# The ring of stored token sums in the down projection: laid out by product, each product's tile fetched after its slot's last product

## The chip, the core and the metric

The kernel runs on one core of a Trainium2 chip. The metric is the device time of one execution in microseconds (us). Three runs of the kernel before took 2399.78, 2400.1 and 2400.78 us; the median is 2400.1 us. Nothing runs on the other cores.

## The reference

One layer of a hybrid decoder trunk is applied to 512 prompt tokens and 8 x 4 sample tokens, in float32, with a model width of 2048 and a hidden width of 8192. The change lies in the MLP, and only there:

```python
h = rms_norm(x, norm_ffn_w[l])
x = x + jnp.square(jax.nn.relu(h @ w_up[l])) @ w_down[l]
```

Ahead of it stands a mixer (a short gated convolution beside a gated delta rule, each behind a large input projection), and behind it a final norm. The 544 token columns are handled as two halves of 272 (`HT`).

## The kernel before

**Numbers.** TensorE (PE) multiplies in a rounded float32 form. So each float32 operand is split into a rounded part `hi` (on ScalarE, ACT) and the rest `lo` (on VectorE, DVE), and each product takes three matmuls: `w_hi` with `x_hi`, `w_hi` with `x_lo`, `w_lo` with `x_hi`. Every matmul there is 128 x 128 by 272 columns.

**Two by two blocks with seven products.** Most of the MLP is done in 2 x 2 blocks in the manner of Strassen and Winograd: two weight blocks by two, times two token halves, with 7 block products in the place of 8. A `Pair` holds the four weight quarters of a block (`w_q`, one DMA each on the queue of SyncE, SP) and builds the sums of weights for the products 6, 5, 7, 3 and 4 on DVE (lines 1118 to 1125). The products run in the order 1, 2, 6, 5, 7, 3, 4 (`ORDER`). For the last sum that the pair needs, `w_s` at line 1120, the quarters `a21` and `a22` must have landed. The weight parts are made two products ahead of PE (`ahead`). An engine works its own instructions in order; the order of the instructions on each engine is set when the kernel is built.

**Way up and way back.** On the way up, each of 32 hidden blocks `m` gives a tile `u` of four parts. For the 28 blocks in `KS` (m from 3 to 30), `keep_sums` makes the seven token sums that the seven products of the way back need, splits each into `hi` and `lo`, and writes all fourteen columns of 272 to a DRAM tensor `ucd{m}`, by four DMAs on the queue of GpSimd (POOL): two for three sums, two for four (lines 1179 and 1180). `T_AT` gives the position `b`, from 0 to 6, of the sum of each product.

On the way back, 42 visits go over the 8 output blocks `m`. A visit multiplies up to six (`SPAN`) consecutive blocks `j` of `KS` into one output block. So a visit of six is 7 products x 6 blocks x 3 matmuls = 126 matmuls. Within a product, PE goes through the blocks `j` in order, the lowest first. Each product's result is added to the output by DVE (line 927).

**The ring.** Only 8 blocks' sums (`RING`) are held in SBUF at a time, seven tiles of 128 x 544 each (`uc`). Where a visit is the last that uses a block `j`, block `j + 8` is fetched into its slots. `last_use` says which visit that is; it is ten visits that fetch, two blocks each. Before the change, the tensor lies as seven `hi` columns and then seven `lo` columns, and tile `b` of a block holds the columns 2b and 2b+1. So one tile serves two products (the `hi` of the products 1 and 3, say), or the `hi` of one and the `lo` of another. The seven DMAs of both blocks are written in the program behind the visit's last product, 4. What waits in fact is each DMA by itself, until PE has read the slot that it fills for the last time. POOL's queue carries nothing else in that part.

**Beginning and end of the ring.** The blocks 0 and 1 are fetched during the last block of the way up (line 1216), the blocks 2 to 7 right behind it (line 1273). Then come eight plain products (`Plain`, hidden block pairs kept aside), four ahead of the first visit and one within each of the first four. Behind the last visit two stored blocks are done with plain products, with their tiles `ux` loaded by SP.

Of the kernel before, what the change touches and what calls it, by code (L numbers as in the profile page):

```python
# [9 lines left out]
F32 = mybir.dt.float32  # L10
# [8 lines left out]
P = 128  # L19
# [38 lines left out]
def trunk(ctx, tc, a):  # L58
# [921 lines left out]
    x2_d = [tile_in(dram, f"x2d{i}", [P, 2, 2, HT]) for i in range(KT // 2)]  # L980
    u_d = {m: tile_in(dram, f"ud{m}", [P, 4, HT]) for m in STORED}
    u0_d = [tile_in(dram, f"u0d{m}", [P, 2, 4, HT]) for m in KEPT]
    uc_d = {m: tile_in(dram, f"ucd{m}", [P, 14, HT]) for m in range(N_PLAIN, NF - 1)}

    first_part(KT - 1, lambda: None)
    ln_exp(True)
# [184 lines left out]
    def keep_sums(m, u):  # L1171

        t = t_tile("tc", "T")
        sums(t, u[:, 1], u[:, 0], u[:, 3], u[:, 2])
        d = uc_d[m]
        for src, at, n in ((u[:, 1:4], 0, 3), (t, 3, 4)):
            hi = t_tile("u_hi", "hi", F32R)[:, :n]
            parts_into(hi, src.bitcast(F32R), src)
            nc.gpsimd.dma_start(d[:, at : at + n], hi.bitcast(F32))
            nc.gpsimd.dma_start(d[:, 7 + at : 7 + at + n], src)  # L1180

    u_0, x2v = [], []

# [5 lines left out]
    def block_out(m):  # L1189
        u = t_tile("u", "u")  # L1190

        def out(p, ps):
            with urgent():
                if p in (1, 6, 5):
                    S.activation(u[:, {1: 1, 6: 0, 5: 2}[p]], ps, AF.Copy)
                elif p == 4:
                    S.activation(u[:, 3], ps, AF.Relu)
                    S.activation(u, u, AF.Square)
                else:
                    d = u[:, {2: 1, 7: 2, 3: 0}[p]]  # L1200
                    V.tensor_tensor(d, d, ps, ADD)
                if p == 3:
                    S.activation(u[:, 0:3], u[:, 0:3], AF.Relu)
            if p == 4 and m in STORED:
                nc.gpsimd.dma_start(u_d[m], u)
            elif p == 4:
                keep_sums(m, u)
            if p == 1 and m == NF - 1:
                residual(range(4), nc.sync)
            if p == 2 and m == NF - 1:  # L1210
                for i in range(4):
                    parts = [c_tile(hlp, "u0") for _ in range(2)]
                    for j in range(2):
                        nc.sync.dma_start(parts[j].bitcast(F32), u0_d[i // 2][:, j, 2 * (i % 2) : 2 * (i % 2) + 2])
                    u_0.append(tuple(parts))
            if p in (6, 5) and m == NF - 1:
                fetch(6 - p)

        return out

    ring = {}
    KS = list(range(N_PLAIN, NF - 1))

    def fetch(j):
        n = {3: 0, 4: 0, 5: 0, 7: 4}.get(j % RING, 7)
        n2 = n + {3: 7, 4: 7}.get(j % RING, 0)
        ring[j] = [c_tile(hlp if b < n else cmb if b < n2 else cmb2, "uc") for b in range(7)]
        for b, t in enumerate(ring[j]):
            nc.gpsimd.dma_start(t.bitcast(F32), uc_d[KS[j]][:, 2 * b : 2 * b + 2])  # L1229

    quad = lambda n, i: gx_tile(i, "w_q", [P, 1024])[:, :n]
    ups = [Pair([a["w_up"][m, q] for q in range(4)], 1024, quad, m) for m in range(N_PLAIN, NF)]
# [25 lines left out]

    qp = pool("q", 6)
    def combos(j):  # L1260
        at = lambda b: ring[j][b // 2][:, b % 2]
        return {p: (at(b), at(7 + b)) for p, b in T_AT.items()}

    visits = [(m, 0, RAMP[m]) for m in range(8) if RAMP[m]]
    at = list(RAMP)
# [4 lines left out]
                visits.append((m, at[m], n))  # L1270
                at[m] += n
    last_use = {j: max(i for i, (m, k0, n) in enumerate(visits) if k0 <= j < k0 + n) for j in range(len(KS))}
    for j in range(2, RING):
        fetch(j)

    def down_out(key):
        v, (m, k0, n) = key
# [2 lines left out]
        def out(p, ps):  # L1280
            for b, h in {1: [(0, 0)], 2: [(0, 0)], 6: [(0, 1)], 5: [(1, 1)], 7: [(1, 1)], 3: [(0, 1)], 4: [(1, 0)]}[p]:
                add(x[:, b, h], ps)
            if p == 4:
                for j in range(len(KS) - RING):
                    if last_use[j] == v:
                        fetch(j + RING)

        return out

# [207 lines left out]
```

## Time and profile before

| | |
|---|---|
| median of 3 runs | 2400.1 us |
| the profiled execution | 2399.76 us |
| its span | 2398.0 us |
| PE busy | 2375.6 us, 99% |
| DVE busy | 1788.5 us, 75% |
| ACT busy | 1054.3 us, 44% |
| POOL busy | 446.6 us, 19% |
| fetches `uc<-ucd` | 196 DMAs of 272 KB, median 5.3 us to landing |
| `w_q` loads of the way back | 128 DMAs of 384 KB, median 3.4 us to landing |

A profile is one execution of the kernel, with a record of each instruction and each DMA. Its span runs from the first to the last record; 1.76 us of the execution's time lie outside. "Idle before" of a group is the time in which its engine did nothing ahead of its instructions, with what ended the wait. Times of an instruction in the text are counted from the start of the span, or with a plus sign from the start of a visit. The way up with stored sums runs from about 1085 to 1685 us, the visits from 1709 to 2332 us.

### The profile page before, as it was taken

The numbers are of one execution on the slowest core, as the hardware profiler recorded it, in microseconds if no ns is written. First come the engines' busy times: TensorE is split into PE (matmuls) and PEld (weight loads), VectorE is DVE, ScalarE is ACT, GpSimd is POOL, SyncE is SP. The second block draws the span as 40 slices with busy tenths as digits, with TensorE's granted clock in tenths as the row PEclk, the third lists the DMA queues.
The fourth block names the chain that finished last, engine by engine and source line by source line (L and its number), as shares of the span: only waits on it lengthen the run. The fifth ranks groups of instructions, "written<-read, shape, count | busy, mean of one in ns | idle before, by whom it ended". The sixth has DMA issues, their size and how long they took to land.

```text
span 2398.0 us, 47088 instructions
## 1 busy us (share of the span) xinstructions
PE 2375.6 (99%) x19089; PEld 2355.9 (98%) x19089; DVE 1788.5 (75%) x2900; ACT 1054.3 (44%) x1548; POOL 446.6 (19%) x727
## 2 busy tenths in 40 slices
PE   9999999999999999999999999999999999999997
PEld 9999999999999999999999999999999999999997
DVE  8676676666658635688888888887587887788885
ACT  6425333432532423355555555555233333333445
POOL 1233223312412302100111001111401112121003
PEclk9999999999999999999999999999999999999999
DMA  6343333333333544345555555556945657564433
GB/s 206 98 120 116 103 112 111 112 100 97 127 95 106 177 129 135 126 159 209 204 188 186 193 193 191 204 201 218 378 139 178 210 165 236 164 224 152 125 98 110
DMA packets 139889, 383.26 MB, mean 160 GB/s; under 512 B 34548, under 2 KB 43416, under 8 KB 139672
## 3 DMA queue, kind: packets, MB, share of 16 engines
q1 hardware_dynamic: 104472, 251.41, 33.2%
q0 software_dynamic: 35056, 128.82, 14.5%
q8 instruction: 150, 2.46, 0.4%
q14 instruction: 67, 0.55, 0.1%
q10 hardware_dynamic: 144, 0.03, 0.0%
HBM read 302.69 MB, written 77.49 MB: 159 GB/s over the span
## 4 chain that ended last, share of the span: by engine, by line
PE 93%; DMA 3%; DVE 2%; ACT 1%; issue 1%; POOLq 0%; SPq 0%; DVEq 0%; POOL 0%; ACTq 0%
PE ps_s L76 48%; PE ps_big L76 38%; PE ps_sm L76 7%; DMA w_q<-in_w_d_dram 1%; DMA ud<-u 1%; DVE w_lo L1130 0%; ACT w_hi L1129 0%; PE ps_sm L80 0%; DMA w_raw<-in_w_first_dram 0%; DMA w_raw<-in_w_d_dram 0%; DVE x2v L927 0%; DVE w_lo L146 0%; DVE ssq L260 0%; DMA uc<-ucd 0%; ACT w_hi L143 0%
## 5 line engine op out<-in xcount | busy, mean ns | idle before, releaser
L1129 ACT ACTIVATE w_hi<-w_q 128x768 fp32r<-128x768 f32 (+3 forms) x422 | 375.4, 890 | 559.7 <-PE ps_s L76 466.3
L76 PE MATMUL ps_s<-uc,w_hi 128*128 128x272 f32 x3136 | 592.3, 288 | 3.8 <-DVE x2v L927 1.9
L76 PEld LDWEIGHTS ps_s<-uc,w_hi 128*128 128x128 f32 x3136 | 491.2, 188 | 7.2 <-issue 3.8
L76 PE MATMUL ps_big<-x_hi,w_hi 128*128 128x272 f32 x2272 | 479.1, 292 | 0.8 <-ACT x_hi L158 0.6
L1130 DVE TENSOR_TENSOR w_lo<-w_q,w_hi 128x768 fp32r<-128x768 f32 (+3 forms) x422 | 425.5, 1009 | 72.3 <-ACT w_hi L1129 70.2
L76 PE MATMUL ps_big<-x_lo,w_hi 128*128 128x272 f32 x2272 | 472.8, 289 | 0.0
L76 PE MATMUL ps_big<-x_hi,w_lo 128*128 128x272 f32 x2272 | 470.4, 288 | 0.0
L76 PE MATMUL ps_s<-uc,w_lo 128*128 128x272 f32 x1568 | 450.5, 288 | 0.0
L143 ACT ACTIVATE w_hi<-w_raw 128x1024 fp32r<-128x1024 f32 (+3 forms) x187 | 181.7, 972 | 437.0 <-PE ps_big L76 352.4
L76 PEld LDWEIGHTS ps_big<-x_hi,w_hi 128*128 128x128 f32 x2272 | 357.1, 188 | 4.7 <-issue 1.4
L76 PEld LDWEIGHTS ps_big<-x_lo,w_hi 128*128 128x128 f32 x2272 | 357.5, 189 | 0.2 <-DVE x_lo L161 0.2
L76 PEld LDWEIGHTS ps_big<-x_hi,w_lo 128*128 128x128 f32 x2272 | 355.5, 188 | 0.3 <-DVE w_lo L146 0.2
L146 DVE TENSOR_TENSOR w_lo<-w_raw,w_hi 128x1024 fp32r<-128x1024 f32 (+3 forms) x187 | 237.7, 1271 | 106.1 <-ACT w_hi L143 97.3
L76 PEld LDWEIGHTS ps_s<-uc,w_lo 128*128 128x128 f32 x1568 | 295.1, 188 | 0.0
L76 PE MATMUL ps_s<-c_hi,w_hi 128*128 128x272 f32 x928 | 267.3, 288 | 0.4 <-ACT w_hi L1129 0.4
L76 PE MATMUL ps_s<-c_hi,w_lo 128*128 128x272 f32 x928 | 267.5, 289 | 0.0
L76 PE MATMUL ps_s<-c_lo,w_hi 128*128 128x272 f32 x928 | 266.3, 287 | 0.0
L927 DVE TENSOR_TENSOR x2v<-x2v,ps_s 128x272 f32<-128x272 f32 x326 | 140.0, 434 | 65.2 <-PE ps_s L76 64.0
L1229 POOL DMA_DIRECT2D uc<-ucd x196 | 106.6, 548 | 430.2 <-PE ps_s L76 412.7
L76 PEld LDWEIGHTS ps_s<-c_hi,w_hi 128*128 128x128 f32 x928 | 174.9, 188 | 0.7 <-ACT w_hi L1129 0.6
L76 PEld LDWEIGHTS ps_s<-c_hi,w_lo 128*128 128x128 f32 x928 | 174.3, 188 | 0.1
L76 PEld LDWEIGHTS ps_s<-c_lo,w_hi 128*128 128x128 f32 x928 | 174.4, 188 | 0.0
(371 smaller groups left out, 3754.3 us busy)
## 6 DMA issues: line engine op xcount, KB each, us to landing
w_q<-in_w_up_dram SPq DMA_DIRECT2D x116, 512.0 KB, 5.0
w_raw<-in_w_in_dram SPq DMA_DIRECT2D x106, 512.0 KB, 3.4
uc<-ucd POOLq DMA_DIRECT2D x196, 272.0 KB, 5.3
w_q<-in_w_d_dram SPq DMA_DIRECT2D x128, 384.0 KB, 3.4
ucd<-u_hi POOLq DMA_DIRECT2D x28, 544.0 KB, 5.7
ucd<-tc POOLq DMA_DIRECT2D x28, 544.0 KB, 6.8
ucd<-u_hi POOLq DMA_DIRECT2D x28, 408.0 KB, 3.0
ucd<-u POOLq DMA_DIRECT2D x28, 408.0 KB, 2.7
```

The lines of the kernel that those rows point to most:

```text
L76: return cls.held(nc.tensor.matmul(*args, **kw))
L143: S.activation(hi[:, c], raw[:, c], AF.Copy)
L146: V.tensor_tensor(lo[:, c], raw[:, c], hi[:, c].bitcast(F32), SUB)
L927: V.tensor_tensor(out, out, ps, ADD)
L1129: S.activation(hi, s, AF.Copy)
L1130: V.tensor_tensor(lo, s, hi.bitcast(F32), SUB)
L1229: nc.gpsimd.dma_start(t.bitcast(F32), uc_d[KS[j]][:, 2 * b : 2 * b + 2])
```

## The change

The tensor `ucd{m}` is laid out as seven pairs `hi`, `lo`, one pair for each product. So the writes of `keep_sums` put their three or four columns at every second place. A fetched tile `b` holds both parts of one product's sum and nothing else. `fetch` takes a list of blocks and a list of products, and goes product by product, both blocks in each. In a visit that fetches, it is called behind each product with that product alone, in the place of once behind product 4. The first blocks, 0 to 7, are fetched in pairs too, by product.

```diff
-    uc_d = {m: tile_in(dram, f"ucd{m}", [P, 14, HT]) for m in range(N_PLAIN, NF - 1)}
+    uc_d = {m: tile_in(dram, f"ucd{m}", [P, 7, 2, HT]) for m in range(N_PLAIN, NF - 1)}
...
-            nc.gpsimd.dma_start(d[:, at : at + n], hi.bitcast(F32))
-            nc.gpsimd.dma_start(d[:, 7 + at : 7 + at + n], src)
+            nc.gpsimd.dma_start(d[:, at : at + n, 0], hi.bitcast(F32))
+            nc.gpsimd.dma_start(d[:, at : at + n, 1], src)
...
-            if p in (6, 5) and m == NF - 1:
-                fetch(6 - p)
+            if p == 6 and m == NF - 1:
+                fetch((0, 1))
...
-    def fetch(j):
-        n = {3: 0, 4: 0, 5: 0, 7: 4}.get(j % RING, 7)
-        n2 = n + {3: 7, 4: 7}.get(j % RING, 0)
-        ring[j] = [c_tile(hlp if b < n else cmb if b < n2 else cmb2, "uc") for b in range(7)]
-        for b, t in enumerate(ring[j]):
-            nc.gpsimd.dma_start(t.bitcast(F32), uc_d[KS[j]][:, 2 * b : 2 * b + 2])
+    def fetch(js, ps=ORDER):
+
+        for b in (T_AT[p] for p in ps):
+            for j in js:
+                n = {3: 0, 4: 0, 5: 0, 7: 4}.get(j % RING, 7)
+                n2 = n + {3: 7, 4: 7}.get(j % RING, 0)
+                t = c_tile(hlp if b < n else cmb if b < n2 else cmb2, "uc")
+                ring.setdefault(j, {})[b] = t
+                nc.gpsimd.dma_start(t.bitcast(F32), uc_d[KS[j]][:, b])
...
-        at = lambda b: ring[j][b // 2][:, b % 2]
-        return {p: (at(b), at(7 + b)) for p, b in T_AT.items()}
+        return {p: (ring[j][b][:, 0], ring[j][b][:, 1]) for p, b in T_AT.items()}
...
-    for j in range(2, RING):
-        fetch(j)
+    for j in range(2, RING, 2):
+        fetch((j, j + 1))
...
-            if p == 4:
-                for j in range(len(KS) - RING):
-                    if last_use[j] == v:
-                        fetch(j + RING)
+            fetch([j + RING for j in range(len(KS) - RING) if last_use[j] == v], [p])
```

The order of PE, DVE, ACT and SP in the visits stays as it was, but for the loads of `ux` near the end, which SP asks for a weight load earlier, and their split, which ACT and DVE take a few products earlier. What moves is on POOL. The first place is the first visit that fetches (blocks 8 and 9, hidden blocks 11 and 12). POOL asked before for all of one block and then all of the other; the numbers behind `uc` are those of the tiles:

```order
L1229 DMA uc_21636<-ucd11_10337 128x544
L1229 DMA uc_21637<-ucd11_10337 128x544
L1229 DMA uc_21638<-ucd11_10337 128x544
L1229 DMA uc_21639<-ucd11_10337 128x544
L1229 DMA uc_21640<-ucd11_10337 128x544
L1229 DMA uc_21641<-ucd11_10337 128x544
L1229 DMA uc_21642<-ucd11_10337 128x544
L1229 DMA uc_21650<-ucd12_10338 128x544
```

Three of the ten visits had that order (blocks 8 and 9, 16 and 17, 24 and 25). In the seven others POOL took turns between the two blocks for some or most of the first tiles already before; what decides is which slots the scheduler finds free first. So in the second visit that fetches (blocks 10 and 11), whose rows of before are:

```order
L1229 DMA uc_22018<-ucd13_10339 128x544
L1229 DMA uc_22032<-ucd14_10340 128x544
L1229 DMA uc_22019<-ucd13_10339 128x544
L1229 DMA uc_22033<-ucd14_10340 128x544
L1229 DMA uc_22020<-ucd13_10339 128x544
```

and this is the same place of the kernel after:

```order
L1232 DMA uc_21878<-ucd13_10339 128x544
L1232 DMA uc_21880<-ucd14_10340 128x544
L1232 DMA uc_21906<-ucd13_10339 128x544
L1232 DMA uc_21908<-ucd14_10340 128x544
L1232 DMA uc_21933<-ucd13_10339 128x544
```

The number of DMAs and their size are as before; the tiles' numbers now lie far apart, since each pair is asked for behind another product. In the kernel after, all ten visits take turns in this way.

The second place is POOL's writes of the sums on the way up, here for the first stored block, with the lines of before ahead of those of after:

```order
L1179 DMA ucd_10329<-u_hi 128x816
L1180 DMA ucd_10329<-u 128x816
L1179 DMA ucd_10329<-u_hi 128x1088
L1180 DMA ucd_10329<-tc 128x1088
```

```order
L1179 DMA ucd_10329<-u_hi 128x3x272
L1180 DMA ucd_10329<-u 128x3x272
L1179 DMA ucd_10329<-u_hi 128x4x272
L1180 DMA ucd_10329<-tc 128x4x272
```

The four DMAs stand where they stood; each row of 816 or 1088 floats is now written in three or four pieces of 272.

## The prediction

> **What bounds the kernel now.** I read the page first, then the waits of PE, then the way back visit by visit, and last the DMAs in a visit that loses time. The page gives the span, the busy time of the engines, and the chain that ended last:
>
> ```profile
> span 2398.0 us, 47088 instructions
> PE 2375.6 (99%) x19089; PEld 2355.9 (98%) x19089; DVE 1788.5 (75%) x2900; ACT 1054.3 (44%) x1548; POOL 446.6 (19%) x727
> PE 93%; DMA 3%; DVE 2%; ACT 1%; issue 1%; POOLq 0%; SPq 0%; DVEq 0%; POOL 0%; ACTq 0%
> ```
>
> PE is the bound, and its matmuls are not changed in number or order. So the change can only move the 22.4 us in which PE is not busy, and the slow starts behind them. Fetches of the ring show up in the chain only through what they do to others. The next view takes the ten visits of the way back that fetch, as stretches (the first numbers are the stretch, its length, and PE's busy time with its matmuls):
>
> ```profile
> 1815.63:1831.41 15.78, 15.78 (x128) 15.78 (x127) 12.39 (x19) 5.93 (x7) 6.97 (x13) 1.00 0.65 223
> 1847.21:1863.73 16.52, 16.05 (x128) 15.86 (x127) 12.54 (x19) 5.92 (x7) 6.45 (x12) 1.00 0.68 229
> ...
> 1975.40:1991.19 15.79, 15.79 (x128) 15.79 (x127) 12.44 (x19) 5.93 (x7) 6.97 (x13) 1.00 0.65 215
> ...
> 2134.89:2150.66 15.77, 15.77 (x128) 15.77 (x127) 12.44 (x19) 5.93 (x7) 6.95 (x13) 1.00 0.65 219
> 2198.07:2213.99 15.92, 15.92 (x128) 15.83 (x127) 12.54 (x19) 5.93 (x7) 4.67 (x9) 1.00 0.66 219
> sum 161.42, PE 159.41 PEld 158.19 DVE 124.12 ACT 59.30 POOL 64.17; mean PE 15.94 PEld 15.82 DVE 12.41 ACT 5.93 POOL 6.42
> ```
>
> Ten other visits of six blocks that ask for nothing, from the same view:
>
> ```profile
> 1831.41:1847.21 15.80, 15.80 (x128) 15.80 (x127) 13.12 (x19) 5.93 (x7) 0.63 (x2) 1.00 0.67 225
> ...
> sum 157.93, PE 157.93 PEld 157.93 DVE 131.33 ACT 59.31 POOL 5.89; mean PE 15.79 PEld 15.79 DVE 13.13 ACT 5.93 POOL 0.59
> ```
>
> A visit without requests takes 15.79 us, which is 126 matmuls at 0.125 us. The ten that fetch take 161.42 - 157.93 = 3.49 us more together. That is all that fetching costs now. It doesn't fall on all ten. The three visits in which POOL asks for one block after the other (first, fifth and ninth row of the ten: 15.78, 15.79, 15.77) lose nothing. The seven others take 161.42 - 47.34 = 114.08 us, so 114.08 - 7 x 15.79 = 3.55 us over, 0.51 us each.
>
> Where in the visit? The timeline of DVE at `w_s`, the first sum of the next visit's weights, in a visit without requests (from 1831.41), one that loses (from 1847.21, with the next two instructions), and one that fetches and doesn't lose (from 1975.40); idle time ahead stands in brackets:
>
> ```profile
> 1841.33 0.96 DVE L1120 TENSOR_TENSOR w_s<-w_q 128x768 f32<-128x768 f32 x1 [0.23 <-DMA w_q<-in_w_d_dram]
> ...
> 1858.19 0.96 DVE L1120 TENSOR_TENSOR w_s<-w_q 128x768 f32<-128x768 f32 x1 [1.31 <-DMA w_q<-in_w_d_dram]
> 1859.06 0.95 DVE L1130 TENSOR_TENSOR w_lo<-w_q,w_hi 128x768 fp32r<-128x768 f32 x1
> 1859.93 0.95 DVE L1123 TENSOR_TENSOR w_q<-w_q 128x768 f32<-128x768 f32 x1
> ...
> 1985.62 0.96 DVE L1120 TENSOR_TENSOR w_s<-w_q 128x768 f32<-128x768 f32 x1 [0.57 <-DMA w_q<-in_w_d_dram]
> ```
>
> DVE stands at `w_s` until the last quarter `w_q` of the next visit has landed. Behind `w_s` on DVE are queued the `w_lo` of this visit's own products and the additions that free PE's banks. A wait of 0.57 us is still hidden; one of 1.31 us costs the visit 16.52 - 15.79 = 0.73 us. So about 0.6 us are free, and the rest goes to PE one to one. How long this `w_q` takes is seen in the DMA view of stretches of 0.1 us, at 1837.8, 1853.6 and 1981.8 us (each some 6.45 us into its visit); then the `w_q` asked for at 1855.9, 8.7 us into the losing visit; and last the ring's first tile there, asked for at 1852.55:
>
> ```profile
> w_q<-in_w_d_dram SPq DMA_DIRECT2D x1, 384.0 KB, 3.4
> ...
> w_q<-in_w_d_dram SPq DMA_DIRECT2D x1, 384.0 KB, 4.4
> ...
> w_q<-in_w_d_dram SPq DMA_DIRECT2D x1, 384.0 KB, 3.7
> ...
> w_q<-in_w_d_dram SPq DMA_DIRECT2D x1, 384.0 KB, 4.9
> ...
> uc<-ucd POOLq DMA_DIRECT2D x1, 272.0 KB, 3.1
> ```
>
> The last column is the time to landing: 3.4 us without fetches, 3.7 us without a loss, 4.4 us with one of 0.73. Cost of a fetching visit = landing of the `w_q` of +6.45 us, less 3.7 us. This is the one number on which the change acts.
>
> **The change part by part.** First the requests in a visit. POOL's timeline in the losing visit (start, length, count):
>
> ```profile
> 1852.55 1.09 POOL L1229 DMA_DIRECT2D uc<-ucd  x2 [20.51 <-PE ps_s L76]
> 1854.69 1.09 POOL L1229 DMA_DIRECT2D uc<-ucd  x2 [1.05 <-PE ps_s L76]
> 1857.08 1.09 POOL L1229 DMA_DIRECT2D uc<-ucd  x2 [1.30 <-PE ps_s L76]
> 1859.21 1.63 POOL L1229 DMA_DIRECT2D uc<-ucd  x3 [1.05 <-PE ps_s L76]
> 1862.17 2.17 POOL L1229 DMA_DIRECT2D uc<-ucd  x4 [1.33 <-PE ps_s L76]
> ```
>
> The requests are written behind the visit's last product, but they go out as slots come free: two at +5.34, two at +7.48, two at +9.87, then seven and one more behind. So the burst is there, from the third product on. A product takes 15.79 / 7 = 2.26 us, and the two oldest blocks are read in its first 6 of 18 matmuls, 0.75 us. Third product: 2 x 2.26 + 0.75 = 5.26, seen as 5.34. With one tile for each product, all seven slots come free in this way: at +0.83, 3.09, 5.34, 7.60, 9.86, 12.1 and 14.4 us, two tiles each, the second 0.54 us behind the first. Removed is the crowd behind +12; added are the pairs at +0.83 and +3.09; those at +5.34 and +7.5 stay as they are. The critical `w_q` goes out at +6.45 between just these two. So what it meets is not taken away. The pair of +3.09, 544 KB, is new ahead of it, and by the 3.1 us that the undisturbed tile took its second tile is through at 3.09 + 0.54 + 3.1, about +6.7, when the `w_q` has yet to move data. My forecast is that this request lands as it does now in the visits where POOL takes turns. The three visits that ask for one block whole change to turns too. Ten visits at 0.51 us are 5.1 us, in the place of 3.49: +1.6 us. The bounds: nothing lost in any visit, -3.5 us; all ten like the `w_q` of +8.71, which now has two pairs ahead and one behind, at 4.9 us: 10 x 1.2 = 12 us, +8.5 us. I take the value near the low end since the +6.45 request keeps its own neighbours.
>
> A rule bears on the high end. The Trainium skill, "DMA: Bandwidth & Descriptors", section "Queues, rings and completion order", says that each DMA engine takes turns between the queues that have work for it, packet by packet. By it a `w_q` that meets a full ring queue all the way gets half the rate; with the page's 435 GB/s that is an estimate of 0.9 us on top of the undisturbed 3.4, so 4.3 us, and 10 x 0.6 = 6 us lost in place of 3.49: +2.5 us, which is the forecast within 1 us. The trace has 4.4 us, and 4.9 us for the later request, so here it doesn't stop at that bound.
>
> The other `w_q` of a visit now meet other pairs. SP's requests in the losing visit, and all waits of PE from 1676 to 2335 us:
>
> ```profile
> 1849.68 10.69 SPq L1110 DMA_DIRECT2D w_q<-in_w_d_dram  x4
> ...
> PE ps_s L76 <- DVE x2v L927: 1.9, 5, 0.6
> PE ps_s L76 <- ACT w_hi L1129: 1.6, 4, 0.7
> PE ps_s L76 <- ACT u L1195: 0.3, 1, 0.3
> PE ps_s L76 <- DVE w_lo L146: 0.3, 1, 0.3
> ```
>
> The quarter asked for at 1849.68 is needed at `w_s` too, and even at 4.9 us it lands at 1854.6, well ahead of the critical one; the other two of the four are asked for in the visit before. I cost that at nothing. A late tile of the ring costs nothing either: its first use is three visits later, and PE waits for no `uc` DMA.
>
> Second, the writes on the way up, in pieces of 272. POOL's groups by form: a DMA with twice the rows of 1088 bytes (256x1x272), and one of today's writes:
>
> ```profile
> L1073 POOL DMA_DIRECT2D ud<-u x2 | 1.4, 756 | 21.4 <-ACT u L1063 21.4
> ...
> L1179 POOL DMA_DIRECT2D ucd<-u_hi x56 | 30.4, 543 | 393.2 <-ACT u_hi L988 389.5 <-issue 3.2 <-ACT u L1195 0.5
> ```
>
> 128 more pieces cost 756 - 543 = 213 ns of POOL. With 384 and 512 pieces in the place of 128 that is 0.43 and 0.64 us more; 28 x 2 x (0.43 + 0.64) = 60 us of POOL in all. POOL has them free, as the stretch of the way up shows (third pair from the right: POOL busy), and ACT, which waits for the first write before it can fill `u_hi` again, has its own room:
>
> ```profile
> 1105.00:1676.00 571.00, 570.72 (x4553) 570.12 (x4552) 476.32 (x541) 333.11 (x409) 60.30 (x112) 1.00 0.57 198
> ...
> ACT w_hi L1129 <- PE ps_s L76: 513.0, 372, 2.9
> ...
> ACT u_hi L988 <- DMA ucd<-u_hi: 12.2, 6, 2.9
> ```
>
> ACT waits 513 us for PE and 12.2 us for these writes. 0.43 us later is covered in all blocks but one. At the end of the way up the 2.9 us wait reaches PE:
>
> ```profile
> 1673.27 1.11 ACT L988 ACTIVATE u_hi<-tc 128x1088 fp32r<-128x1088 f32 x1 [2.92 <-DMA ucd<-u_hi]
> ...
> 1675.66 0.39 PE L76 MATMUL ps_s<-d_hi,w_hi 128*128 128x272 f32 x1 [0.28 <-ACT u L1195]
> ```
>
> There I add 0.4 us. Bounds: 0, and if the cover were gone, 0.43 in each of 28 blocks, 12 us.
>
> Third, the first loads: the same 56 DMAs at the same places in POOL's queue, with the pair that is needed first asked for first. PE doesn't wait for them now. Nothing, either way. The `ux` loads near the end go out a weight load earlier, as their slots come free earlier: nothing.
>
> Sum: 1.6 + 0.4 = +2.0 us on the profiled execution's own 2399.76 us (span 2398.0 and 1.76 around it). It lies 0.3 us below the median, so 2400.1 + 2.0 = 2402.1 us.
>
> **The rivals.** *The `w_q` gets free.* With the load spread over the whole visit, the critical request lands in 3.7 us or less. For it: three visits already do this with the same two pairs around it, and the crowd is thinner. Against it: the pairs at +5.34 and +7.48 stay, and the seven lost already with nothing else in flight. Price: -3.5 + 0.4 = -3.1 us, 2397.0.
>
> *A steady queue (slower).* With pairs every 2.26 us the ring's queue is never empty when the critical request comes; its place is now like that of the +8.71 request. If it lands in 4.55 us on average, half way between 4.2 (0.51 + 3.7) and 4.9, ten visits lose 0.85 us, 8.5 in place of 3.49: +5.0, with 0.4 2405.5 us. It decides from the point at which the pair of +3.09 isn't through at +6.7. For it: the DMA share of a fetching visit is 0.65 already, and it is now spread over its whole length. Against it: what matters is the neighbours, and these are the same.
>
> *The pieces bite.* Writes in 1088-byte pieces land so late that each block's second `u_hi` holds up ACT as the last one does: 0.4 us in each of 28 blocks, 12 us, and 1.6: 2413.7. For it: one such wait has reached PE. Against it: ACT's 513 us of room.
>
> *It does not do what it says.* The scheduler already gave out slots as they came free, so the pairs stay where they are: 2400.1. Against it: a tile with two products' parts can't come free after the first product.
>
> **How the numbers follow.** Forecast 0.5, the free `w_q` 0.22, the steady queue 0.18, the pieces 0.05, no effect 0.05. What a measurement can tell from no change is 0.2%, 4.8 us: from 2395.3 to 2404.9 counts as the same. All of the forecast, the free `w_q` but for 0.03 (should the first loads gain as well), no effect, and a third of the steady queue lie in it: 0.50 + 0.19 + 0.05 + 0.06 = 0.80; above lie 0.12 + 0.05 = 0.17; below 0.03. The predicted time is that of the likeliest, 2402.1. The range reaches from the free `w_q`, 2397.0 less 0.5, to the steady queue and 1 us more for its unknown landing: 2396.5 to 2406.5.
>
> **What would show it.** In the profile after: POOL's requests in pairs at +0.8, 3.1, 5.3, 7.6, 9.9, 12.1 and 14.4 us of each fetching visit; the `w_q` of +6.45 landing in 4.1 to 4.6 us; the ten visits together at about 163 us; waits of DVE at `w_s` of about 1.1 us in all ten, the three free ones among them. POOL's writes on the way up at about 0.97 and 1.18 us each. Wrong would be: ten visits at 157.9 us, or above 166; a way up that is longer; a PE that waits for `uc`.

## The result and the profile after

The kernel after takes 2418.03 us (median of 6 runs, 2414.29 to 2422.25), the kernel before in the same set 2401.06 us (6 runs, 2399.78 to 2403.92). The ratio is 1.0074, with a 95% interval of 1.0062 to 1.0086: 17 us slower. Timed again in the second set of experiments (e5 below) it took 2421.18 us, ratio 1.009 (1.0077 to 1.0103). The forecast was 2402.1 us with a range to 2406.5; it was wrong.

The profiled execution of the kernel after took 2416.35 us. Its page gives the span, and the waits of PE from the end of the way up to the end of the visits follow:

```profile
span 2414.6 us, 47088 instructions
```

```profile
PE ps_s L76 <- DVE x2v L927: 15.0, 9, 2.3
PE ps_s L76 <- ACT w_hi L1129: 2.4, 5, 0.9
PE ps_s L76 <- ACT u L1195: 0.7, 1, 0.7
```

The wait for DVE's additions (line 927) has gone from 1.9 us in 5 times to 15.0 us in 9 times. The ten visits that fetch, as stretches with their sum, and then the visit right behind the first of them:

```profile
1816.09:1833.57 17.48, 16.01 (x129) 15.82 (x127) 12.33 (x19) 5.92 (x7) 7.46 (x14) 1.00 0.82 284
1849.36:1866.90 17.54, 16.04 (x129) 15.85 (x128) 12.47 (x19) 5.92 (x7) 7.47 (x14) 1.00 0.85 283
...
2146.36:2163.23 16.87, 16.01 (x129) 15.82 (x128) 12.30 (x19) 5.92 (x7) 7.47 (x14) 1.00 0.85 284
2210.60:2230.44 19.84, 17.55 (x128) 17.36 (x127) 13.76 (x19) 5.92 (x7) 7.47 (x14) 0.91 0.81 269
sum 177.56, PE 161.75 PEld 159.85 DVE 124.97 ACT 59.23 POOL 74.64; mean PE 16.17 PEld 15.99 DVE 12.50 ACT 5.92 POOL 7.46
```

```profile
1833.57:1849.36 15.79, 15.79 (x128) 15.79 (x127) 13.24 (x19) 5.93 (x7) 0.00 (x0) 1.00 0.45 135
```

The ten take 177.56 us in the place of 161.42, so 16.1 us of the 16.6 us by which the span grew are here. All ten lose; before, three lost nothing. The last two columns show what moved: the DMA share within a fetching visit rose from between 0.65 and 0.69 to between 0.81 and 0.85, and in the visit behind the first of them it fell from 0.67 to 0.45. What that visit moved fell from 225 to 135 GB/s over 15.79 us, 1.4 MB of the 3.9 MB (14 x 272 KB) that a visit asks for. The bytes of the kernel are the same. A third of the ring's traffic has moved from the visit behind, which lost nothing by carrying it, into the fetching visit, where the two new pairs (1.1 MB) go out ahead of the critical `w_q`.

DVE in the second fetching visit, which starts at 1849.36:

```profile
1858.59 0.44 DVE L927 TENSOR_TENSOR x2v<-x2v,ps_s 128x272 f32<-128x272 f32 x1 [0.55 <-PE ps_s L76]
1861.36 0.96 DVE L1120 TENSOR_TENSOR w_s<-w_q 128x768 f32<-128x768 f32 x1 [2.34 <-DMA w_q<-in_w_d_dram]
1862.23 0.95 DVE L1130 TENSOR_TENSOR w_lo<-w_q,w_hi 128x768 fp32r<-128x768 f32 x1
1863.10 0.95 DVE L1123 TENSOR_TENSOR w_q<-w_q 128x768 f32<-128x768 f32 x1
1863.97 0.43 DVE L927 TENSOR_TENSOR x2v<-x2v,ps_s 128x272 f32<-128x272 f32 x1
```

DVE stands 2.34 us at `w_s` where it stood 1.31 us, and the next addition, which frees a bank for PE, comes behind three instructions (`w_s`, a `w_lo` and a `w_q`), 2.6 us after `w_s` starts. POOL's requests in this visit:

```profile
1850.20 1.07 POOL L1232 DMA_DIRECT2D uc<-ucd  x2 [16.98 <-PE ps_s L76]
1852.45 1.06 POOL L1232 DMA_DIRECT2D uc<-ucd  x2 [1.18 <-PE ps_s L76]
1854.71 1.06 POOL L1232 DMA_DIRECT2D uc<-ucd  x2 [1.19 <-PE ps_s L76]
1856.96 1.07 POOL L1232 DMA_DIRECT2D uc<-ucd  x2 [1.19 <-PE ps_s L76]
```

They stand at +0.84, 3.09, 5.35 and 7.60, as forecast. The DMA view of stretches of 0.1 us, at 1851.76 (the `w_q` of +2.40), 1852.45, 1854.71 (the pairs of +3.09 and +5.35, the first tile of each) and 1855.81 (the critical `w_q` of +6.45); the last column is the time to landing:

```profile
w_q<-in_w_d_dram SPq DMA_DIRECT2D x1, 384.0 KB, 5.0
...
uc<-ucd POOLq DMA_DIRECT2D x1, 272.0 KB, 4.6
...
uc<-ucd POOLq DMA_DIRECT2D x1, 272.0 KB, 5.0
...
w_q<-in_w_d_dram SPq DMA_DIRECT2D x1, 384.0 KB, 5.5
```

Everything is late from +2.4 on. The critical `w_q` needs 5.5 us (4.8 to 6.3 over the ten visits), where it needed 3.7 to 4.4 in the visits quoted of before.

The rest of the loss is on the way up. POOL's writes of `u` and of `tc` there took 0.547 and 0.539 us in the kernel before. In the kernel after, in three pieces and in four, they took:

```profile
L1180 POOL DMA_DIRECT2D ucd<-u x28 | 21.2, 757 | 122.2 <-DVE u L989 106.7 <-DVE u L1201 15.5
L1180 POOL DMA_DIRECT2D ucd<-tc x27 | 20.3, 753 | 17.7 <-DVE tc L989 17.5 <-issue 0.2
```

DVE's wait at `w_s` for the `w_q` of the way up, first in the kernel before, then in the kernel after:

```profile
DVE w_s L1120 <- DMA w_q<-in_w_up_dram: 22.2, 24, 2.4
```

```profile
DVE w_s L1120 <- DMA w_q<-in_w_up_dram: 38.2, 24, 3.0
```

In this execution the first product behind the way up starts 0.7 us later than before (1685.5 for 1684.75 us). In the other profiles with writes in pieces this part is 3.4 to 6.0 us.

### The profile page after: what moved, and what is told of

The parts are those of the page before. It is cut to its first block, busy times and chain, and to the rows that moved or that the text cites. A ratio compares the mean times of both kernels' runs of the same rounds, so it can differ in the third digit from the quotient of the medians.

```text
span 2414.6 us, 47088 instructions
## 1 busy us (share of the span) xinstructions
PE 2378.4 (99%) x19089; PEld 2357.6 (98%) x19089; DVE 1788.4 (74%) x2900; ACT 1053.4 (44%) x1548; POOL 466.4 (19%) x727
## 4 chain that ended last, share of the span: by engine, by line
PE 68%; issue 22%; POOL 3%; DMA 3%; DVE 2%; ACT 1%; POOLq 0%; SPq 0%; DVEq 0%; ACTq 0%
PE ps_big L76 38%; PE ps_s L76 23%; PE ps_sm L76 7%; DMA w_q<-in_w_d_dram 2%; POOL ucd L1179 2%; POOL ucd L1180 2%; DVE w_lo L1130 1%; ACT w_hi L1129 0%; PE ps_sm L80 0%; DVE x2v L927 0%; DVE w_q L1123 0%; DMA ud<-u 0%; DMA ucd<-u_hi 0%; DMA xr<-in_x_dram 0%; ACT tmp L254 0%
```

## The experiments

Each of the twelve kernels was timed beside the kernel before. "Ten" is the sum of the ten visits that fetch, "behind" that of the ten visits right behind them, "way up" the time of the first product behind the way up against the kernel before's profile (1684.75 us). The kernel before has 161.42, 157.91 and 0.

| run | median us | ratio to before, interval | ten | behind | way up |
|---|---|---|---|---|---|
| after (first set) | 2418.03 | 1.0074 (1.0062, 1.0086) | 177.56 | 157.86 | +0.7 |
| e5 after again | 2421.18 | 1.009 (1.0077, 1.0103) | 181.87 | 158.57 | +3.4 |
| e1 layout only | 2417.09 | 1.0076 (1.0063, 1.0088) | 171.38 | 157.97 | +6.0 |
| e6 read in pieces | 2413.43 | 1.0059 (1.0046, 1.0073) | 176.07 | 158.59 | -0.5 |
| e7 write in pieces | 2404.04 | 1.0017 (1.0008, 1.0026) | 161.26 | 158.91 | +3.8 |
| e2 one later | 2406.14 | 1.0024 (1.0014, 1.0034) | 158.44 | 163.73 | +3.5 |
| e3 quiet | 2421.57 | 1.0091 (1.0078, 1.0105) | 158.52 | 178.46 | +5.2 |
| e4 sum later | 2410.09 | 1.0041 (1.0027, 1.0055) | 160.12 | 159.97 | +3.6 |
| e9 no first | 2426.34 | 1.0109 (1.0095, 1.0122) | 171.22 | 174.05 | +1.8 |
| e10 no second | 2426.87 | 1.0108 (1.0094, 1.0122) | 168.78 | 175.04 | -0.6 |
| e11 no both | 2429.57 | 1.0121 (1.0106, 1.0137) | 159.21 | 189.66 | +1.6 |
| e12 write delay | 2417.52 | 1.0072 (1.0059, 1.0085) | 161.44 | 157.88 | +14.3 |
| e8 two visits | 2396.29 | 0.999 (0.9981, 0.9998) | 157.81 | 158.35 | -0.5 |

### What asks early: the layout or the place of the call?

e1 is the kernel after, with all requests written behind product 4 again:

```diff
-            fetch([j + RING for j in range(len(KS) - RING) if last_use[j] == v], [p])
+            if p == 4:
+                fetch([j + RING for j in range(len(KS) - RING) if last_use[j] == v])
```

> The kernel after, but all seven requests of a block are again written behind the visit's last product, as before the change; layout and one-product tiles stay. Theory (a steady queue: the tiles of one product come free early, so the pairs of about +0.9 and +3.2 go out early whatever line asks for them): POOL's requests stand where they stand in the kernel after, the ten visits sum to about 177 us, and the time is that of the kernel after, 2417 to 2418 us. Rival (the place of asking does it): requests go back to +5.3 and later, ten visits at 161 to 163 us, 2401 us.

The time is that of the kernel after, and POOL's seven pairs stand where they stand in it. The ten visits lost 13.5 us in this profile, less than forecast, and the way up 6.0. So it is the tiles of one product that bring the requests forward; the line that asks changes nothing about when the requests go out.

### The two halves of the change, apart

e6 keeps after's tiles and requests, but lays the tensor out as before, so that the writes are whole and each tile is read in two pieces:

```diff
-    uc_d = {m: tile_in(dram, f"ucd{m}", [P, 7, 2, HT]) for m in range(N_PLAIN, NF - 1)}
+    uc_d = {m: tile_in(dram, f"ucd{m}", [P, 14, HT]) for m in range(N_PLAIN, NF - 1)}
...
-                nc.gpsimd.dma_start(t.bitcast(F32), uc_d[KS[j]][:, b])
+                nc.gpsimd.dma_start(t.bitcast(F32), uc_d[KS[j]][:, b : b + 8 : 7])
```

> The kernel after with the tensor laid out as before (seven hi, then seven lo): the writes of the way up go in whole rows again, and each tile of the ring is read in two pieces of 1088 bytes per partition. The requests of the ring stay as in the kernel after. Theory (two costs: early pairs in the visits, pieces in the writes): the end of the way up comes as in the kernel before, within 0.7 us; the ten visits stay at 170 to 178 us; in all 2411 to 2416 us. Rival (reads in pieces load the queues more): the ten visits at 180 us or more, 2420 us or more. Rival (the writes cost nothing): the time of the kernel after.

e7 is the kernel before, with after's layout and its writes in pieces, but with each tile shared by two products so that slots come free when they did before:

```diff
+            nc.gpsimd.dma_start(d[:, at : at + n, 0], hi.bitcast(F32))
+            nc.gpsimd.dma_start(d[:, (at + 4) % 7 : (at + 4) % 7 + n, 1], src)
...
+        return {p: (ring[j][b][:, 0], ring[j][(b + 4) % 7][:, 1]) for p, b in T_AT.items()}
```

> The kernel before, with the sums written in the pieces of the kernel after: the tensor is laid out as seven pairs, but a pair holds the hi of one product's sum and the lo of another's, so chosen that the slots come free at the same points as before. Requests, their order and every other instruction as before. Theory (early pairs cost the visits, pieces cost the way up): the ten visits at 161 to 163 us, with the first pair at +5.3; the end of the way up late by 1 to 6 us; in all 2401.5 to 2406 us. Rival (the layout slows the reads too): visits at 165 us or more. Rival (pieces cost nothing, the late way up of the first set had another cause): 2400 us.

And e5 is the kernel after once more, beside them:

> The kernel after, unchanged, profiled once more beside the three others of this set. In the first set four kernels with the way up of the kernel after came to its end 3.3 to 6.0 us later than the kernel before; the profile of the kernel after shows only 0.6. Theory (the writes of the sums in pieces delay the w_q of the way up, and how much differs from run to run): the end of the way up is again 3 to 6 us late, the ten visits sum to 168 to 178 us, in all 2414 to 2422 us. Rival (the way up is as in the first profile of after): 0.6 us late.

The sums of the ten visits, of e6 and then of e7:

```profile
sum 176.07, PE 162.59 PEld 160.69 DVE 125.89 ACT 59.26 POOL 98.13; mean PE 16.26 PEld 16.07 DVE 12.59 ACT 5.93 POOL 9.81
```

```profile
sum 161.26, PE 160.08 PEld 158.47 DVE 123.69 ACT 59.29 POOL 64.28; mean PE 16.01 PEld 15.85 DVE 12.37 ACT 5.93 POOL 6.43
```

Against the 2399.64 us of before in this set, the requests alone cost 13.8 us, the writes alone 4.4, both 21.5. So in this set both together cost 3.3 us more than the sum of the halves, 18.2; in the first set, at 17.0 us, they cost 1.2 less. The ten visits of e5 came to 181.87 us, above what was expected of it. The kernel is the same that took 177.56 before, and the difference is the slower clock of the last section: it cost 1.7 us in the first profile and 6.1 in e5, and without it both lost 17.9 us. Both halves are as the theory had them. In the visits nothing is left for the layout itself: with before's requests, e7's ten visits are before's. Of e7's 4.4 us, 3.8 lie on the way up in the profile and 1.0 in one visit behind.

How DVE's wait at `w_s` on the way up reaches PE is seen in e5. From 1080 to 1692 us PE and its weight loads wait 2.8 us for `u` and 2.0 for `w_lo`; in the kernel before it is 1.2 us and none. That is 3.6 us more, for a way up that ended 3.4 us late. The two largest of these waits in e5:

```profile
PEld ps_s L76 <- ACT u L1195: 2.0, 6, 1.0
PEld ps_s L76 <- DVE w_lo L1130: 1.8, 5, 0.4
```

### Where does the delay go if the requests come later?

In e2 and e3 a small copy on POOL, which waits for the addition of the product before, holds the requests back. The table gives, for each product of the visit, whose pairs go out behind it:

```diff
+            ps_now = {1: (), 2: (1,), 6: (2,), 5: (6,), 7: (5, 7), 3: (3, 4), 4: ()}[p]   # e2
+            ps_now = {1: (), 2: (), 6: (), 5: (1, 2), 7: (6, 5), 3: (7, 3), 4: (4,)}[p]   # e3
...
+                    V.tensor_copy(f[:, :1], x[:, b, h, :1])
+                tc.keep_in_program_order(G.tensor_copy(f[:, 1:], f[:, :1]))
+                fetch(js, ps_now, True)
```

> The kernel after, with its layout, but POOL may ask for product 1's pair only behind product 2, for product 2's behind 6, 6's behind 5, then 5's and 7's behind 7, 3's and 4's behind 3: the first pair at about +5.1, the next at 7.4 and 9.7, four requests each at 11.9 and 14.2. That is about the pattern of the kernel before around the w_q of +6.5. Theory (the pairs of +0.9 and +3.2 are what delays this w_q): it lands in 4.1 to 4.6 us again, ten visits at 161 to 163 us, 2401 to 2402 us. Rival (the new layout itself reads slower, or one pair just ahead is enough): the w_q stays at 5 us or more, ten visits at 170 us or more, 2409 us or more. What the layout costs on the way up (0.4 to 0.6 us) stays in.

> The kernel after, but POOL asks for no tile of the ring before about +9.7 of a fetching visit: the pairs of products 1 and 2 go out behind product 5, those of 6 and 5 behind 7, of 7 and 3 behind 3, that of 4 behind 4. Theory: the w_q of +6.5 has the queues to itself and lands in 3.4 to 3.7 us, no fetching visit loses there, ten visits at 158 to 159 us, 2397 to 2398 us, below both kernels. Rival (the crowd then meets the first w_q of the next visit's weights, asked for from +8.8 on and in the next visit at +2.4, and the loss only moves there): the loss stays at 3.5 us or more, 2401 us or more, with DVE's wait at another sum than w_s, or in the visit behind.

The gates opened later than planned: e2's first pair went out at +6.4 in place of 5.1, e3's at +11.6 in place of 9.7. The fetching visits became all but free of loss in both, 0.5 and 0.6 us in the ten. But in both the loss came back in the visit behind, in e3 in full:

```profile
sum 158.52, PE 158.52 PEld 158.52 DVE 130.57 ACT 59.29 POOL 47.99; mean PE 15.85 PEld 15.85 DVE 13.06 ACT 5.93 POOL 4.80
sum 178.46, PE 162.29 PEld 160.39 DVE 127.53 ACT 59.25 POOL 49.07; mean PE 16.23 PEld 16.04 DVE 12.75 ACT 5.92 POOL 4.91
```

The first is e3's ten, the second the ten behind. In the first visit behind in e3 the crowd's last request went out at +4.7, and DVE waited for the critical `w_q`, asked for at 1845.39 us (+6.45), with `w_s` right after it:

```profile
w_q<-in_w_d_dram SPq DMA_DIRECT2D x1, 384.0 KB, 5.3
...
1850.74 0.96 DVE L1120 TENSOR_TENSOR w_s<-w_q 128x768 f32<-128x768 f32 x1 [2.14 <-DMA w_q<-in_w_d_dram]
```

It is the same cost as in a fetching visit: 5.3 - 3.7 = 1.6 us by the landing, 17.33 - 15.79 = 1.54 measured.

So e3's rival was right: a gap around one `w_q` only moves the loss, if the fourteen requests then go out in a crowd. The theory had 2401 to 2402 us for e2 and 2397 to 2398 for e3; both times missed it, e2 by the 5.8 us that its visits behind lost and by its way up.

### Does the loss pass through `w_s`?

e4 is the kernel after, with the sum `w_s` built one product later in DVE's order, for the visits from 6 on:

```diff
-                if p == 6:
+                if p == (2 if self.soon else 6):
                     self.s1 = tile_in(rawp, "w_s1", [P, 1024], tag="w_raw")[:, :n]
                     s1 = V.tensor_tensor(self.s1, a21, a22, ADD)
```

> The kernel after with all its requests as they are; only the sum w_s, which waits for the last w_q, stands one product later in DVE's order (two products ahead of product 2's use in place of product 1's), for the visits from 6 on. Theory (the loss reaches PE only because DVE stands at w_s with other work queued behind it): the w_q lands as late as in the kernel after, 5 to 6 us, but DVE does not wait at w_s, the ten visits fall from 177.6 to 158 to 160 us, 2398 to 2401 us. Rival (PE waits for what the fetches do to other loads, or the later sum makes the weights of product 6 late): the visits stay above 165 us or visits without requests get longer, 2406 us or more.

All waits of PE in e4 from 1800 to 2330 us:

```profile
PE ps_s L76 <- DVE x2v L927: 0.3, 1, 0.3
```

All of PE's waits there but 0.3 us are gone, with POOL's early pairs as in the kernel after. But the SP queue changed with it: some `w_q` are asked for later, and the critical one landed in 3.9 to 5.3 us. In the eighth fetching visit (from 2108.52) it was asked for at 2115.14 and needed the longest:

```profile
w_q<-in_w_d_dram SPq DMA_DIRECT2D x1, 384.0 KB, 5.3
```

In the old order these 5.3 us would cost 1.6. Here `w_s` comes at +14.3 without a wait, and the visit takes 16.02 us like the others of this kernel. So the loss goes through DVE's wait at `w_s`; at 5.5 us, the mean of the kernel after, it was not tried. The order has a price of its own: nearly every visit from 6 to 35, with requests or without, is 0.2 us longer than 15.79, 6 us in all. That was not in the theory. So the time missed the theory's 2398 to 2401 us and came out in the range of the rival, whose condition holds in one part: visits without requests got longer.

One more thing shows here. The `w_q` that the kernel after asks for at +2.4 goes out at +4.18 in e4; the pairs of +0.84 and +3.08 stay. In the ten visits the first tile of the pair of +3.08 then lands in 2.9 to 3.3 us, where it took 4.2 to 5.1 in the kernel after. In the second fetching visit (from 1852.15):

```profile
uc<-ucd POOLq DMA_DIRECT2D x1, 272.0 KB, 2.9
```

So it is above all the `w_q` of +2.4 that holds this pair up.

### Which pair is one too many?

e9, e10 and e11 are e6 with the pairs of product 1, of product 2, or of both held until product 7 has been added:

```diff
+            ps_now = {1: (), 7: (1, 7)}.get(p, (p,))              # e9
+            ps_now = {2: (), 7: (2, 7)}.get(p, (p,))              # e10
+            ps_now = {1: (), 2: (), 7: (1, 2, 7)}.get(p, (p,))    # e11
```

> The kernel of e6 (after's requests, whole writes, reads in two pieces; ten visits 176.1 us, 2413.4 us), but product 1's pair, at +0.9, is held back until product 7 has been added, about +13 of the visit; product 7's own pair goes out behind it. The pairs of +3.1, 5.4 and 7.6 stay. Theory (backlog: each early pair adds to what the w_q of +6.5 finds ahead of it, and the pair of +0.9 does so through the w_q of +2.4): the ten visits fall about half way, 165 to 171 us, the critical w_q at about 4.8 us; 2403 to 2408 us. Rival (only the pair just ahead, that of +3.1, counts): 174 us or more, 2411 us or more. Rival (any two pairs ahead are free, the third is too much): 161 to 163 us.

> The kernel of e6, but product 2's pair, at +3.1, is held back until product 7 has been added, about +13; product 7's own goes out behind it. The pairs of +0.9, 5.4 and 7.6 stay. Theory (backlog): the ten visits at 162 to 168 us, no more than with the pair of +0.9 held back, since the queue can run empty between +4.5 and +5.4; 2400 to 2405 us. Rival (the pair of +0.9, which meets the w_q of +2.4, is what counts): 172 us or more, 2409 us or more.

> The kernel of e6, but the pairs of product 1 and of product 2 are both held back until product 7 has been added, and product 7's goes out behind them: six requests at about +13 in the place of those at +0.9, 3.1 and 9.9. Around the w_q of +6.5 stand the pairs of the kernel before, +5.4 and +7.6. Theory: the ten visits at 160 to 163 us as before, 2399 to 2402 us, or a little more where the tail of the six delays the next visit's w_q. Rival (tiles of one product or reads in two pieces are slow in themselves): 168 us or more, 2406 us or more.

The edit did something else than those texts say. A new tile takes whichever slot is free first, so the pair next in the order took the held pair's slot. POOL in the third fetching visit of e9 (from 1887.52) and of e11 (from 1886.60):

```profile
1888.36 1.41 POOL L1232 DMA_DIRECT2D uc<-ucd  x2 [13.15 <-PE ps_s L76]
1890.62 1.41 POOL L1232 DMA_DIRECT2D uc<-ucd  x2 [0.85 <-PE ps_s L76]
1892.88 1.41 POOL L1232 DMA_DIRECT2D uc<-ucd  x2 [0.85 <-PE ps_s L76]
1903.30 0.90 POOL L1294 COPY flag<-flag 128x1 f32<-128x1 f32 x1 [9.00 <-DVE flag L1293]
```

```profile
1887.44 1.41 POOL L1232 DMA_DIRECT2D uc<-ucd  x2 [13.16 <-PE ps_s L76]
1889.71 1.41 POOL L1232 DMA_DIRECT2D uc<-ucd  x2 [0.85 <-PE ps_s L76]
1900.48 0.90 POOL L1294 COPY flag<-flag 128x1 f32<-128x1 f32 x1 [9.36 <-DVE flag L1293]
```

So e9 and e10 both have pairs at +0.84, 3.1 and 5.36 and then, in eight of the ten visits, none till +15 to 17; e11 has those of +0.84 and +3.1 alone. In the fourth and the eighth visit of e9 and e10 the second tile of the third pair goes out only at +8.0; there the critical `w_q` landed in 3.7 to 4.2 us, and the visit lost at most 0.5. The crowd behind the held pairs costs the next visits 16 to 32 us, which makes the times useless; the fetching visits are over before it, and tell what the `w_q` of +6.45 met. The losses are over 157.93, the sum of ten visits without requests. The part by the slower clock (last section) is half of PE's busy time at the granted clock of 0.5.

| pairs that go out up to about +10, by kernel | the ten lose, us | by the slower clock | mean landing of the critical `w_q` |
|---|---|---|---|
| none (e3) | 0.6 | 0.8 | 3.2 |
| at most one, +1.1 to 1.9 (e8) | -0.1 | 0 | 3.3 |
| +6.4, +8.7 (e2) | 0.5 | 0 | 3.6 |
| +0.84, 3.1 (e11) | 1.3 | 1.3 | 3.3 |
| +5.34, 7.48 (before; e7) | 3.5; 3.3 | 0; 0 | 4.1; 4.0 |
| +0.84, 3.1, 5.36 (e10; e9) | 10.9; 13.3 | 0; 1.6 | 4.8; 4.9 |
| +0.84, 3.1, 5.35, 7.6 (e1; e6; after; e5) | 13.5; 18.1; 19.6; 23.9 | 1.6; 2.6; 1.7; 6.1 | 4.9; 5.3; 5.5; 5.6 |

Take for each visit what its critical `w_q` needs over 3.7 us, and add up the ten. That gives 18.4 us for the kernel after, 3.7 for before and for e12, 12.3 for e1, 18.8 for e5, 16.0 for e6, 12.1 for e9, 11.2 for e10, 3.5 for e7, and at most 0.2 for the four others. Each lies within 1 us of the loss without the clock's part. (e4 is left out, since its `w_s` stands elsewhere.) So the landing of this one load accounts for the loss in all of them.

The two early pairs alone do no harm (e11). With the pair of +5.35 behind them the `w_q` needs 4.8 to 4.9 us (e9, e10), and with that of +7.6 too, 4.9 to 5.6. No kernel here has the pair of +5.35 by itself; before has it with that of +7.48 and loses 0.35 us a visit. In the second visit of the kernel after, the early pairs and the `w_q` of +2.4 put the pair of +5.35 back so far that its second tile lands at +11.8, while the critical `w_q` is in flight from +6.45 to +11.95.

### Pieces, or a later start of the writes?

e12 is the kernel before, with whole writes, but POOL copies 64 columns of the source ahead of each write:

```diff
+            for to, part in ((at, hi.bitcast(F32)), (7 + at, src)):
+                tc.keep_in_program_order(G.tensor_copy(hold, part[:, 0, :64]))
+                tc.keep_in_program_order(nc.gpsimd.dma_start(d[:, to : to + n], part))
```

> The kernel before, with whole writes, but ahead of each write of the sums POOL copies 64 columns of what it is about to write, at about 0.24 us each, so that each write goes out about as much later as the 0.21 us longer issue of the kernel after makes it. Theory (it is the pieces in the queues that delay the w_q of the way up): the end of the way up as in the kernel before, within 0.7 us, DVE's wait at w_s on the way up 20 to 27 us, 2399 to 2401 us. Rival (the later start of the writes shifts them against the w_q): 3 to 4 us later, DVE's wait at 38 to 46 us, 2403 to 2405 us.

The copies took longer than planned, by POOL's groups on the way up; then DVE's wait there:

```profile
L1181 POOL COPY hold<-tc 128x64 f32<-128x64 f32 x27 | 28.1, 1043 | 12.2 <-DVE tc L990 12.2
L1181 POOL COPY hold<-u_hi 128x64 f32<-128x64 f32 x53 | 26.2, 494 | 287.5 <-ACT u_hi L989 287.5
```

```profile
DVE w_s L1121 <- DMA w_q<-in_w_up_dram: 65.5, 26, 3.7
```

Whole writes that start 0.3 to 1.0 us later, with the copies that delay them, cost 14.3 us on the way up, with the visits as they were. That is far over the 3 to 4 us that the rival had. So no pieces are needed for such harm, and the theory, that it must be the pieces, fell. What the 0.21 us longer issue of the kernel after does by itself, and what its pieces do, is not told apart: the delay could not be made that small here, and the copies also load POOL and hold the sources a little longer.

### A version that beats both

e8 is the kernel before, its layout and its tiles; the seven pairs are spread over two visits with the gates of e2:

```diff
+            for late, tiles in ((0, {5: 1, 7: 5, 3: 2, 4: 0}), (1, {5: 4, 7: 3, 3: 6})):
+                js = [j + RING for j in range(len(KS) - RING) if last_use[j] == v - late]
```

> The kernel before, its layout and its tiles of two products, with the seven pairs of requests held back and spread over two visits: behind the products 5, 7, 3 and 4 of the visit that frees the slots, and behind 5, 7 and 3 of the next, so at about +10, 12.5, 15 and 17.5 us and then +10, 12.5 and 15 us. Theory (a w_q is late when it has more than one pair ahead of it or beside it): no visit loses more than 0.1 us, the ten that fetch and the ten behind them at 158 us each, 2396 to 2397 us, below the kernel before. Rival (any pair in flight delays the w_q of +2.4 and +8.8 enough): as much or more is lost than in the kernel before, 2400 us or more.

The sums of its ten visits and of the ten behind, and DVE's wait at `w_s` (13.7 us in the kernel before):

```profile
sum 157.81, PE 157.81 PEld 157.81 DVE 129.42 ACT 59.30 POOL 49.41; mean PE 15.78 PEld 15.78 DVE 12.94 ACT 5.93 POOL 4.94
sum 158.35, PE 158.03 PEld 157.85 DVE 129.96 ACT 59.30 POOL 69.73; mean PE 15.80 PEld 15.78 DVE 13.00 ACT 5.93 POOL 6.97
```

```profile
DVE w_s L1120 <- DMA w_q<-in_w_d_dram: 6.1, 18, 1.1
```

Both parts came out as expected but for one visit of the ten behind, the last, which lost 0.5 us. 2396.29 us, 3.4 us below the kernel before in the same set, with the interval just short of 1.

## Why the prediction was wrong

- *Cost of a fetching visit = landing of the `w_q` of +6.45 us, less 3.7 us.* Right. Second fetching visit: 5.5 - 3.7 = 1.8 us, measured 17.54 - 15.79 = 1.75. All ten: 18.4 us by this sum, 17.9 measured, with 1.7 us of the slower clock on top, which the prediction did not have.
- *Requests in pairs at +0.83, 3.09, 5.34 and so on.* Right to 0.02 us. That three visits that lost nothing would lose too came true as well. The reason given, that their requests now take turns between two blocks, is not shown: in e12, with the requests at the times of before, the first fetching visit lost 0.92 us (critical `w_q` 4.7 us), where it lost nothing in the kernel before. Why three visits of before go free stays open.
- *"The pair of +3.09 ... is through at about +6.7, when the `w_q` has yet to move data."* This step failed. It took the landing of a tile that nothing disturbs, 3.1 us, for one that comes behind the pair of +0.84 and the `w_q` of +2.40. Its first tile took 4.6 us, to +7.7, the pair of +5.35 then 5.0 us, to +10.4, and both lie beside the critical `w_q` from +6.45 to +11.95. The forecast let the critical `w_q` land in 4.2 us (0.51 + 3.7) as before; it took 5.5 on average, and the ten visits lost 17.9 us by it in place of 5.1.
- *The `w_q` of +2.4 "I cost at nothing".* True of what waits for it, false of what it does: its 384 KB are part of the backlog. In e4, where it goes out at +4.18, the first tile of the pair of +3.08 lands in 2.9 to 3.3 us and the second is through at +6.8 to 7.6, where it is +8.0 to 9.1 in the kernel after. And "what matters is the neighbours, and these are the same" was the reason given against the steady queue; e9 to e11 show that the same neighbours land by what came before them.
- *The value taken.* The steady queue was a rival at 0.18, decided by just the point that came true; its 4.55 us were too low as well, 5.5 was measured, outside the bound of 4.9. The rule of the Trainium skill that was weighed there ("DMA: Bandwidth & Descriptors", section "Queues, rings and completion order": queues with work take turns by packet) led to an estimate of 4.3 us for a ring queue that is full all the way. The ten visits had 4.8 to 6.3 us, so the estimate fails. It counted the ring's queue alone, while the `w_q` of +2.40 was on SP's own queue until +7.4; that the engines take turns is not contradicted by these traces.
- *The writes: 0.97 and 1.18 us of POOL.* Wrong in size, 0.75 us for three pieces and for four. The 0.4 us at the last block came (PE's wait for `u`, line 1195, from 0.3 to 0.7). What was not seen is that the writes share their time with the `w_q` of the way up: I looked for the cost at ACT's wait for `u_hi`, and it was at DVE's wait at `w_s`, 22.2 us before and 38.2 to 46.5 in the seven profiles with pieces. The way up was then 0.7 to 6.0 us late, 3.7 on average. The line is not sharp: of the five other profiles with whole writes and no delay, four had a wait of 14.7 to 28.7 us, but e11, with 28.7, was 1.6 us late, and e9 had 44.9 and was 1.8 late. The profiles differ by up to 1 us already at the start of this stretch. By e7's time the new writes are worth 4.4 us, 1.9 to 6.2 by its interval. Whether their pieces or their later start does it stays open.
- *First loads, `ux`, a ring tile that comes late: nothing.* Right; PE waits for no `uc`, and the last two visits take 12.85 us for 12.81.

## What to carry to other kernels

A transfer's time to landing is not its own property: before taking an undisturbed one from the trace for a request that moves, add up what is asked for ahead of it on every queue and see whether that has drained. Requests that go out as soon as their slots are free can pile up ahead of the one load that matters, as here (DMA share 0.83 in the visit that asks, 0.45 in the one behind); spread them over the stretch in which nothing else is asked for, and away from the one load on which an engine with other work queued stands. A load that an in-order engine waits for in the midst of its queue is the place to look, on the way up as on the way back.

## What the runs showed of the hardware that was not expected

**A wait of 2 us can cost another 1.6.** In e5 the fourth fetching visit (from 1949.23) lost 3.98 us. PE's busy time and, third from the right, the granted clock in four stretches in a row, from the wait on, and then PE's first matmuls behind the wait:

```profile
1962.83:1965.13 2.30, 0.08 (x2) 0.03 (x1) 2.30 (x5) 0.83 (x1) 0.00 (x0) 1.00 1.03 394
1965.13:1965.32 0.19, 0.19 (x1) 0.19 (x2) 0.19 (x1) 0.00 (x0) 0.00 (x0) 1.00 1.06 301
1965.32:1968.73 3.41, 3.41 (x17) 3.41 (x16) 3.34 (x5) 0.00 (x0) 1.07 (x2) 0.50 0.73 246
1968.73:1969.73 1.00, 1.00 (x9) 1.00 (x9) 0.76 (x2) 0.61 (x1) 0.00 (x0) 1.00 0.59 226
```

```profile
1965.13 0.63 PE L76 MATMUL ps_s<-uc,w_hi 128*128 128x272 f32 x2 [2.22 <-DVE x2v L927]
...
1968.50 0.53 PE L76 MATMUL ps_s<-uc,w_hi 128*128 128x272 f32 x2
```

Behind a wait of 2.22 us the granted clock was 0.50 for 3.41 us. Over the visits of all fourteen profiles there are 58 waits of PE of 0.95 to 1.82 us, and none was followed by it; of 26 waits of 1.84 to 2.71 us, 17 were, at a cost of 1.46 to 1.61 us each. That is why the same kernel gave 177.56 and 181.87 us for the ten visits: one such visit in the first profile (the row with 0.91 above), four in the second.

What decides among the 26 is where the wait lies in time. Within one execution the falls of the clock lie whole multiples of 3.4133 us apart, to about 1 ns. In e5 they come at 1965.32, 2033.59, 2101.85 and 2135.99 us, so 20, 20 and 10 such periods apart. On the grid that these falls give, each of the 17 waits has at least 1.84 us within one period. The nine others are cut in two by the border of a period: eight have at most 1.76 us on either side of it, and one, with 1.89 us, is the exception. So of two waits of equal length one can cost 1.5 to 1.6 us more than the other, by where it lies in time. The Trainium skill ("TensorE: Matmul & The Clock Gate", Part 1) has the clock fall after an idle window of about 3.4 us, and its windows run freely, without starting anew with the kernel. The 3.4133 us of the grid and the 3.41 us at the lower clock agree with that length, but the window need not be idle throughout: here 1.84 us of it was enough.

**The issue of a DMA in pieces.** POOL's time for a write rose from 0.54 us for one piece per partition to 0.75 us for three and for four alike; a read of the ring in two pieces took 0.70 us (1.41 for the pair, above). So it grows up to three pieces, and no further with the fourth.
